# Casting the first 256 weight rows of the first feed-forward product last, behind ACT's seventh copy of the embedding projection

## The chip, the cores and the metric

The kernel runs on one core of a Trainium2 chip. A core has a matrix engine (TensorE, in the profile PE, with its weight loads as PEld), a vector engine (VectorE, DVE), an activation engine (ScalarE, ACT), a general engine (GpSimd, POOL) and an engine that here only issues transfers (SyncE, SP); all run their own instruction streams in order and wait for one another by semaphores. Transfers from memory (HBM) are issued by SP, ACT or POOL. The metric is the device time of one execution in microseconds (us), lower is better.

## The reference

One layer of a hybrid attention and recurrent block over 512 tokens of 1024 channels. What concerns us is its second half:

```python
h = layer_norm(DEEPNORM_ALPHA * h + merged @ w_out[l], ln1_g[l], ln1_b[l])
ff = jnp.square(jax.nn.relu(h @ w_ff1[l])) @ w_ff2[l]      # 1024 -> 4096 -> 1024
r = DEEPNORM_ALPHA * h + ff
r = r + jax.nn.sigmoid(r @ w_ple_gate[l]) * (p[l] @ w_ple_proj[l])
h = layer_norm(r, ln2_g[l], ln2_b[l])
```

The product `p[l] @ w_ple_proj[l]` (256 to 1024 channels, the embedding's projection) needs nothing of the layer's other results.

## The kernel before

Products in float32 are made of three matmuls in a reduced float32 format. An operand is split into a high part (a cast, on ACT) and a low part (operand minus high part, mostly on DVE); the product is high x high, high x low and low x high. The stationary operand of a matmul is loaded by a weight load (PEld) ahead of it.

The stretch around the change goes from the output projection (`po`) to the first feed-forward product. PE works, in this order, on the last block of the output projection, eight blocks of the embedding's projection (`ple_projection`, tile `ppw`, six matmuls each, two halves of columns times four blocks of tokens), mixed with transposes of the normed rows `r` (`hps`, by `h_factors`), and then the first product of the first feed-forward matrix. Each `ppw` block is copied by ACT (`pws`) and stored to a buffer in memory by SP (`pwd`). The eight blocks use a ring of three accumulator banks, but for the seventh, which has a bank of its own (`aux`).

`h_factors` makes the activations' factors out of the transposes: copies `hb` and `a22`, high parts `hc0H` to `hc6H` on ACT, low parts `hc0L` to `hc6L` and some sums on DVE. It is called for blocks 0 to 2 of tokens before the stretch, and for two halves of it (block 1 and block 3) inside it.

The first feed-forward product uses Strassen-like sums: columns of `w_ff1` go in four groups of 1024, and in each group seven products P1 to P7 take the place of eight. In the first group PE's order is P1, P2, P3, P5, P7, P6, P4. `w1_factor(t, n)` makes the factors of product n of group t: a weight tile `w1q` has 512 rows as four pieces of 128 partitions (k = 0 to 3) by 512 columns; for each pair of pieces ACT casts 1024 columns to the high part `w1h`, DVE subtracts to the low part `w1l`, and where a later product needs a sum of two weight quarters, POOL issues a transfer that adds the other quarter onto the pair in place (`W1_ADD`). P1 and P5 read the same tile: P5 reads it after P1's adds, P6 after P5's. P3 and P7 share a tile in the same way. The high and low parts have two buffers each, so a product's factors can be written when PE is through with the product two before.

The order of instructions on an engine is that of the program, but for operations that are put behind a named one (`tc.issue_after`); `queued` puts each operation of ACT and DVE in the feed-forward stage behind the last one that `queued` issued on the engine. In the kernel before, P1's factors are made when the fourth `pws` copy has been issued (`stored[0]`), in one piece:

```python
with tc.issue_after(normed[0].ins), tc.issue_after(stored[0].ins):
    w1 = w1_factor(0, P1)
```

`ff1` makes the matmuls of a product: for each of four blocks of 128 columns the 4 pieces k in order with the high weights, against the high and the low activations, and after all those the low weights.

Of the kernel before, what the change touches and what calls it, by code (L numbers as in the profile page):

```python
# [53 lines left out]
def f(ap):  # L54
    return ap.bitcast(F32)
# [3 lines left out]
def block_kernel(ctx: ExitStack, tc: tile.TileContext, t, out):  # L59
    nc = tc.nc  # L60
    te, ve, se, ge, sy = nc.tensor, nc.vector, nc.scalar, nc.gpsimd, nc.sync
# [8 lines left out]
    def open_pool(name, side=None, space=None, reuse="tile"):  # L70
        kw = {}
        if side:
            kw["side"] = side
        if space:
            kw["space"] = space
        cm = tc.tile_pool(name=name, bufs=1, reuse_waits=reuse, **kw)
        p = cm.__enter__()
        return p, (lambda: cm.__exit__(None, None, None))
# [26 lines left out]
    def gtile(name, dtype=F32R, n=None):  # L105

        if n is None:
            n = len(gplaces) % 4
            gplaces.append(n)
        return gpool.tile([P, 4, S], dtype, tag=f"g{n}", bufs=1, name=name)  # L110
# [249 lines left out]
    for i in range(1, NT):  # L360
        n = (i + 1) * P
# [136 lines left out]
    todo = list(dense)  # L498
# [286 lines left out]
    def half_product(ps, sh, sl, ws):  # L785

        for k, (wh, wl) in enumerate(ws):
            mm = mm3(ps, sh(k), sl(k), wh, wl, k == 0, k == len(ws) - 1)
        return mm

    def blocks(ws):
        return [(wh[:, k, :], wl[:, k, :]) for wh, wl in ws for k in range(2)]
# [49 lines left out]
    def queued(engine, op, *args, **kw):  # L842

        if engine in order_of:
            with tc.issue_after(order_of[engine].ins):
                order_of[engine] = getattr(engine, op)(*args, **kw)  # L846
        else:
            order_of[engine] = getattr(engine, op)(*args, **kw)

    order_of = {}  # L850
# [29 lines left out]
    P1, P2, P3, P4, P5, P6, P7 = range(7)  # L880
# [4 lines left out]
    def w1_rows(t, w):  # L885
        c = groups[t] * 1024 + w[1] * 512
        return w_ff1[w[0] * 512:(w[0] + 1) * 512, c:c + 512].rearrange("(k p) c -> p k c", p=P)

    def w1_load(t, w, issue=None):
# [14 lines left out]
        else:  # L904
            loads.append(sy.dma_start(tl, w1_rows(t, w)))

    W1_OF = {P1: B11, P2: B21, P3: B22, P5: B11, P7: B22, P6: B11, P4: B21}

    W1_ADD = {P1: B12, P5: B22, P3: B12}

    def w1_factor(t, n):

        tl = w1q[t, W1_OF[n]]
        hi, lo = (pools[1].tile([P, 4, 512], F32R, tag="w1" + x, bufs=2, name="w1" + x) for x in "hl")
        for k in (slice(0, 2), slice(2, 4)):
            queued(se, "copy", hi[:, k], tl[:, k])
            queued(ve, "tensor_sub", lo[:, k], tl[:, k], f(hi[:, k]))
            if n in W1_ADD:
                ge.dma_start(out=tl[:, k], in_=w1_rows(t, W1_ADD[n])[:, k], accum_op=OP.add)  # L919
        if n == P6:  # L920
            for k in (slice(0, 2), slice(2, 4)):
                queued(ve, "tensor_add", w1q[t, B21][:, k], w1q[t, B21][:, k], tl[:, k])
        return hi, lo
# [9 lines left out]
    pwss, projected, stored = [], [], []  # L933

    def ple_projection(i, hh):

        ps = (aux if (hh, i) == (1, 2) else acc)("ppw")
        tok = slice(i * P, (i + 1) * P)
        projected[:] = [half_product(ps, lambda k: pTH[:, k, tok], lambda k: pTL[:, k, tok], blocks(wp[hh:hh + 1]))]
        if i == 0:  # L940
            pwss.append(gtile("pws", F32))
        pws = pwss[hh][:, i]
        stored[:] = [se.copy(pws, ps)]
        sy.dma_start(pwd[:, i, hh * 512:(hh + 1) * 512], pws)

    todo = [(i, hh) for hh in range(2) for i in range(NT)]
# [3 lines left out]
    with tc.issue_after(normed[0].ins), tc.issue_after(stored[0].ins):  # L950
        w1 = w1_factor(0, P1)
# [4 lines left out]
    with tc.issue_after(projected[0].ins):  # L956
        h_factors(NT - 1)
    with tc.issue_after(turned[0].ins):
        for _ in range(2):
            ple_projection(*todo.pop(0))  # L960
    close_ln()
    close_hb()
    pools[0], close_fb = open_pool("fb", side="right")
# [93 lines left out]
    def rows_of(g, w):  # L1057
        return ff2_rows[w[0], g, :, :, w[1] * 512:(w[1] + 1) * 512]
# [14 lines left out]
    def add(g, tl, w):  # L1073
        return ge.dma_start(out=tl, in_=rows_of(g, w), accum_op=OP.add)  # L1074
# [18 lines left out]
    for k, (t_, n) in enumerate(seq):  # L1093
# [7 lines left out]
        if k + 1 < len(seq):  # L1101
            nxt = w1_factor(*seq[k + 1])
# [31 lines left out]
    late, close_late = open_pool("late", side="left")  # L1134
# [298 lines left out]
```

## Time and profile before

| what | value |
|---|---|
| time, median of 3 runs (lowest to highest) | 769.85 us (769.58 to 770.32) |
| the profiled execution's own time | 769.99 us |
| its span, first to last instruction | 768.3 us |
| PE busy | 757.8 us, 99% of the span |
| DVE, ACT, POOL busy | 596.7, 418.4, 268.1 us |
| mean granted clock of PE | 0.996 of full |

The span is what the trace covers; 1.7 us of the execution's own time lie outside it. All times of events are microseconds from the span's start. A busy share is an average over stages, so it is read by stage below. Matmuls overlap: one of 512 columns is shown 0.39 us long, but the next starts 0.23 us behind it.

### The profile page before, as it was taken

The page shows a single profiled execution, that of the slowest core. Times are in us where ns is not written, and L with a number is a line of the kernel's source. Part 1 is how long each engine was busy: PE and PEld are TensorE (multiplying, and loading weights), DVE is VectorE, ACT ScalarE, POOL GpSimd, SP SyncE. Part 2 cuts the span into 40 slices and gives each one's busy share as a digit, 9 for nine tenths or more (in the row PEclk, how much of TensorE's full clock was granted, in tenths as well). Part 3 has the DMA queues.
Part 4 walks back from the last instruction along what each step waited for, and adds up shares of the span by engine and source line. Part 5 has one row for each costly group of instructions (what it writes and reads, how often), then busy time and mean ns, then how long its engine had stood idle before and what let it go on. Part 6 is the DMA issues. An engine that isn't in the chain of part 4 may idle for free.

```text
span 768.3 us, 11493 instructions
## 1 busy us (share of the span) xinstructions
PE 757.8 (99%) x4332; PEld 663.2 (86%) x4332; DVE 596.7 (78%) x979; ACT 418.4 (54%) x637; POOL 268.1 (35%) x332
## 2 busy tenths in 40 slices
PE   8999999999999999999999999999999999999995
PEld 8788888889988888878889999999988888888885
DVE  7949999965557987585896767576888988998558
ACT  5546466697756633532366556656565465555210
POOL 6654554444255437470232121212010101126341
PEclk9999999999999999999999999999999999999998
DMA  8443233222223112372089996937497799895202
GB/s 283 127 131 83 56 82 83 83 69 68 71 67 92 62 44 81 91 289 101 1 243 200 335 249 191 238 84 129 112 223 192 144 402 305 140 184 186 93 27 110
DMA packets 77544, 110.43 MB, mean 144 GB/s; under 512 B 3248, under 2 KB 38576, under 8 KB 76208
## 3 DMA queue, kind: packets, MB, share of 16 engines
q1 hardware_dynamic: 58992, 72.76, 28.9%
q0 software_dynamic: 13920, 27.27, 20.6%
q10 hardware_dynamic: 4576, 9.67, 3.6%
q8 instruction: 34, 0.56, 0.3%
q14 instruction: 22, 0.18, 0.1%
HBM read 101.29 MB, written 8.39 MB: 143 GB/s over the span
## 4 chain that ended last, share of the span: by engine, by line
PE 94%; DVE 3%; issue 1%; POOL 1%; DMA 1%; DVEq 0%; ACT 0%; POOLq 0%
PE pf L993 21%; PE pf L1224 20%; PE pg L152 5%; PE pg L154 5%; PE pg L153 5%; PE pu L154 2%; PE pu L152 2%; PE pu L153 2%; PE po L152 2%; PE po L154 2%; PE po L153 2%; PE ptp L480 1%; PE kv L285 1%; PE mv L154 1%; PE mv L153 1%
## 5 line engine op out<-in xcount | busy, mean ns | idle before, releaser
L846 DVE TENSOR_TENSOR w1l<-w1q,w1h 128x1024 fp32r<-128x1024 f32 x55 | 65.0, 1222 | 34.8 <-ACT w1h L846 34.4
L846 DVE TENSOR_TENSOR wl<-b,wh 128x2048 fp32r<-128x2048 f32 x28 | 64.8, 2313 | 10.4 <-ACT wh L846 10.4
L846 ACT CAST w1h<-w1q 128x1024 fp32r<-128x1024 f32 x55 | 55.3, 1048 | 23.6 <-PE pf L993 20.6
L919 POOL DMA_DIRECT2D w1q<-in_w_ff x24 | 29.2, 1254 | 111.7 <-DVE w1l L846 108.4
L145 POOL TENSOR_TENSOR wgl<-wgr,wgh 128x256 fp32r<-128x256 f32 x64 | 49.9, 813 | 47.5 <-ACT wgh L142 47.5
L1074 POOL DMA_DIRECT2D b<-in_w_ff x14 | 17.9, 1279 | 133.3 <-DVE wl L846 125.6
L1224 PE MATMUL pf<-wh,ah 128*128 128x512 f32 x216 | 58.1, 391 | 0.0
L1224 PE MATMUL pf<-wh,al 128*128 128x512 f32 x216 | 57.8, 389 | 0.0
L846 ACT CAST wh<-b 128x2048 fp32r<-128x2048 f32 x28 | 53.5, 1909 | 3.2 <-DMA b<-in_w_ff 3.2
L1224 PE MATMUL pf<-wl,ah 128*128 128x512 f32 x216 | 53.5, 390 | 0.0
L154 PE MATMUL pg<-xH,wgl 128*128 128x512 f32 x128 | 50.6, 395 | 0.0
L152 PE MATMUL pg<-xH,wgh 128*128 128x512 f32 x128 | 50.4, 394 | 0.0
L153 PE MATMUL pg<-xL,wgh 128*128 128x512 f32 x128 | 50.3, 393 | 0.0
L1224 PEld LDWEIGHTS pf<-wh,al 128*128 128x128 f32 x216 | 40.6, 188 | 8.5
L1224 PEld LDWEIGHTS pf<-wh,ah 128*128 128x128 f32 x216 | 40.3, 188 | 8.7 <-ACT wh L846 0.4
L1224 PEld LDWEIGHTS pf<-wl,ah 128*128 128x128 f32 x216 | 40.5, 188 | 8.4
L145 POOL TENSOR_TENSOR wul<-wur,wuh 128x128 fp32r<-128x128 f32 x64 | 36.6, 605 | 19.0 <-ACT wuh L142 19.0
L846 DVE TENSOR_TENSOR c<-c,pf 128x512 f32<-128x512 f32 x48 | 30.5, 683 | 10.2 <-ACT c L846 10.2
L846 ACT ACTIVATE c<-c 128x1024 f32<-128x1024 f32 x12 | 12.7, 1061 | 31.3 <-DVE c L846 31.3
L767 POOL TENSOR_TENSOR lag<-lag,mhalf 128x1 f32<-128x1 f32 x8 | 7.5, 941 | 61.1 <-DVE lag L766 61.1
L153 PEld LDWEIGHTS pg<-xL,wgh 128*128 128x128 f32 x128 | 24.1, 188 | 4.6
L152 PEld LDWEIGHTS pg<-xH,wgh 128*128 128x128 f32 x128 | 24.1, 188 | 4.5
(396 smaller groups left out, 2297.1 us busy)
## 6 DMA issues: line engine op xcount, KB each, us to landing
b<-in_w_ff POOLq DMA_DIRECT2D x14, 1024.0 KB, 9.1
w1q<-in_w_ff POOLq DMA_DIRECT2D x24, 512.0 KB, 7.6
w1q<-in_w_ff SPq DMA_DIRECT2D x9, 1024.0 KB, 7.6
wgr<-in_w_in SPq DMA_DIRECT2D x16, 512.0 KB, 3.8
b<-in_w_ff SPq DMA_DIRECT2D x8, 1024.0 KB, 7.0
wor<-in_w_out SPq DMA_DIRECT2D x8, 512.0 KB, 7.3
b<-in_w_ff ACTq DMA_DIRECT2D x4, 1024.0 KB, 8.8
wpgr<-in_w_ple_gate SPq DMA_DIRECT2D x8, 512.0 KB, 9.1
```

Source lines behind the costliest of these rows:

```text
L145: (lo_eng or ge).tensor_sub(lo[:, k:k + n], raw[:, k:k + n], f(hi[:, k:k + n]))
L152: te.matmul(ps, sh, mh, start=first, stop=False, **kw)
L153: te.matmul(ps, sh, ml, start=False, stop=False, **kw)
L154: return te.matmul(ps, sl, mh, start=False, stop=last, **kw)
L285: te.matmul(b1[i][:, :208], (xH, xL, xH)[kind][:, k, i * P:(i + 1) * P], (wh, wh, wl)[kind], start=k == 0 and kind == 0, stop=k == KD - 1 ...
L480: te.transpose(ps[:, slot * P:(slot + 1) * P], prs[slot // 2][:, slot % 2, j * P:(j + 1) * P], ident)
L767: ge.tensor_tensor(out=ag[:, 3:4], in0=ag[:, 2:3], in1=mhalf[:, 0:1], op=OP.pow))
L846: order_of[engine] = getattr(engine, op)(*args, **kw)
L919: ge.dma_start(out=tl[:, k], in_=w1_rows(t, W1_ADD[n])[:, k], accum_op=OP.add)
L993: mm = te.matmul(ps, w[:, k, b * P:(b + 1) * P], a[:, k], start=fresh, stop=w is lo and k == 3, skip_group_check=True)
L1074: return ge.dma_start(out=tl, in_=rows_of(g, w), accum_op=OP.add)
L1224: mm = te.matmul(banks[n, s], (al if kind == 1 else ah)[:, q, tok], (wl if kind == 2 else wh)[:, q], start=fresh and kind == 0 and q == 0, ...
```

## The change

The casts, subtractions and adding transfers of P1 of the first group are split. The second pair of pieces (rows 256 to 511) is handled where P1's factors were made before. The first pair (rows 0 to 255) is handled in `finish`, which is called between the seventh and the eighth block of the embedding's projection and puts its cast behind ACT's copy of the seventh block. All later casts of the stage, P2's first, are queued behind that cast. The instructions are the same in number and shape.

```diff
+    late = []
...
-        for k in (slice(0, 2), slice(2, 4)):
+        def part(k):
             queued(se, "copy", hi[:, k], tl[:, k])
             queued(ve, "tensor_sub", lo[:, k], tl[:, k], f(hi[:, k]))
+
+        def add(k):
             if n in W1_ADD:
                 ge.dma_start(out=tl[:, k], in_=w1_rows(t, W1_ADD[n])[:, k], accum_op=OP.add)
+
+        if t == 0 and n == P1:
+
+            part(slice(2, 4))
+            add(slice(2, 4))
+
+            def finish(wait):
+                with tc.issue_after(wait.ins):
+                    order_of[se] = se.copy(hi[:, 0:2], tl[:, 0:2])
+                queued(ve, "tensor_sub", lo[:, 0:2], tl[:, 0:2], f(hi[:, 0:2]))
+                add(slice(0, 2))
+
+            late.append(finish)
+        else:
+            for k in (slice(0, 2), slice(2, 4)):
+                part(k)
+                add(k)
...
     with tc.issue_after(turned[0].ins):
-        for _ in range(2):
-            ple_projection(*todo.pop(0))
+        ple_projection(*todo.pop(0))
+        late.pop()(stored[0])
+        ple_projection(*todo.pop(0))
```

On ACT, from the first cast of P1 on, the rows of before are these (`w1h_4380` is P1's high part, `w1h_4476` P2's, `w1h_4530` P3's):

```order
L848 CAST w1h_4380<-w1q_4280 128x1024 [waits DMAHW2_49,Activation_49]
L846 CAST w1h_4380<-w1q_4280 128x1024
L846 CAST w1h_4476<-w1q_4312 128x1024 [waits DMAHW3_49,Activation_49]
L846 CAST w1h_4476<-w1q_4312 128x1024
L810 COPY hb1_3977<-hps1_4326 128x4x128 [waits PE_49]
L114 CAST hc1H_3949<-hps1_4326 128x4x128
L943 COPY pws_4397<-ppw_4390 128x512 [waits PE_49]
L943 COPY pws_4397<-ppw_4400 128x512 [waits PE_49]
L814 COPY a22_4419<-hps1_4410 128x512 [waits PE_49,Activation_49]
L114 CAST hc2H_3958<-hps1_4410 128x4x128
L943 COPY pws_4397<-ppw_4437 128x512 [waits PE_49]
L943 COPY pws_4397<-ppw_4446 128x512 [waits PE_49]
```

and of the change, up to the same last copy:

```order
L848 CAST w1h_4380<-w1q_4280 128x1024 [waits DMAHW2_49,Activation_49]
L810 COPY hb1_3977<-hps1_4326 128x4x128 [waits PE_49]
L114 CAST hc1H_3949<-hps1_4326 128x4x128
L964 COPY pws_4394<-ppw_4387 128x512 [waits PE_49]
L964 COPY pws_4394<-ppw_4397 128x512 [waits PE_49]
L814 COPY a22_4416<-hps1_4407 128x512 [waits PE_49,Activation_49]
L114 CAST hc2H_3958<-hps1_4407 128x4x128
L964 COPY pws_4394<-ppw_4434 128x512 [waits PE_49]
L932 CAST w1h_4380<-w1q_4280 128x1024
L846 CAST w1h_4476<-w1q_4312 128x1024 [waits DMAHW3_49,Activation_49]
L846 CAST w1h_4476<-w1q_4312 128x1024
L964 COPY pws_4394<-ppw_4446 128x512 [waits PE_49]
```

Three casts moved behind six copies and casts of the factors and the projection; the eighth copy now stands behind them.

On DVE the low parts of P1 and P2 (`w1l_4381`, `w1l_4477`) stood ahead of the factors of the last block of tokens:

```order
L848 TENSOR_TENSOR w1l_4381<-w1q_4280,w1h_4380 128x1024 [waits DMAHW2_49,Activation_49]
L846 TENSOR_TENSOR w1l_4381<-w1q_4280,w1h_4380 128x1024 [waits Activation_49]
L846 TENSOR_TENSOR w1l_4477<-w1q_4312,w1h_4476 128x1024 [waits DMAHW3_49,Activation_49]
L846 TENSOR_TENSOR w1l_4477<-w1q_4312,w1h_4476 128x1024 [waits Activation_49]
L120 TENSOR_TENSOR hc1L_3950<-hps1_4326,hc1H_3949 128x4x128 [waits PE_49,Activation_49]
L120 TENSOR_TENSOR hc2L_3959<-hps1_4410,hc2H_3958 128x4x128 [waits PE_49,Activation_49]
L817 TENSOR_TENSOR hps1_4410<-hps0_4409,a22_4419 128x512 [waits DVE_49]
L820 TENSOR_TENSOR hps2_4424<-hps1_4410,hb0_3976 128x512 [waits DVE_49]
L824 TENSOR_TENSOR hps0_4409<-hb0_3976,hps0_4409 128x512
L821 TENSOR_TENSOR hps3_4425<-hps2_4424,hb1_3977 128x512 [waits DVE_49]
```

and with the change:

```order
L848 TENSOR_TENSOR w1l_4381<-w1q_4280,w1h_4380 128x1024 [waits DMAHW2_49,Activation_49]
L120 TENSOR_TENSOR hc1L_3950<-hps1_4326,hc1H_3949 128x4x128 [waits PE_49,Activation_49]
L120 TENSOR_TENSOR hc2L_3959<-hps1_4407,hc2H_3958 128x4x128 [waits PE_49,Activation_49]
L817 TENSOR_TENSOR hps1_4407<-hps0_4406,a22_4416 128x512 [waits DVE_49]
L820 TENSOR_TENSOR hps2_4421<-hps1_4407,hb0_3976 128x512 [waits DVE_49]
L824 TENSOR_TENSOR hps0_4406<-hb0_3976,hps0_4406 128x512
L846 TENSOR_TENSOR w1l_4381<-w1q_4280,w1h_4380 128x1024 [waits Activation_49]
L821 TENSOR_TENSOR hps3_4422<-hps2_4421,hb1_3977 128x512 [waits DVE_49]
L846 TENSOR_TENSOR w1l_4477<-w1q_4312,w1h_4476 128x1024 [waits DMAHW3_49,Activation_49]
L846 TENSOR_TENSOR w1l_4477<-w1q_4312,w1h_4476 128x1024 [waits Activation_49]
```

P1's second subtraction and P2's two stand behind the factors' sums; POOL's transfer into rows 0 to 255 waits for the former.

On PE the order is the same; these are the rows of the change where P1 starts, the last of the eighth projection block ahead of it:

```order
L154 MATMUL ppw_4446<-wp_4277,pT_4264 128x512
L1015 MATMUL pf_4466<-hc0H_3947,w1h_4380 128x256 [waits Activation_49]
L1015 MATMUL pf_4466<-hc0H_3947,w1h_4380 128x256 x3
L1015 MATMUL pf_4466<-hc0L_3948,w1h_4380 128x256 x4
L1015 MATMUL pf_4466<-hc0H_3947,w1h_4380 128x256 x4
L1015 MATMUL pf_4466<-hc0L_3948,w1h_4380 128x256 x4
```

The first matmul of P1 (line 993 before, 1015 now) waits for ACT, now for the late cast.

## Rows read from the trace of the kernel before

**Rows 1.** The page: busy time, share of the span and instructions of each engine; and the engines' shares of the chain of work that ended last.

```profile
PE 757.8 (99%) x4332; PEld 663.2 (86%) x4332; DVE 596.7 (78%) x979; ACT 418.4 (54%) x637; POOL 268.1 (35%) x332
...
PE 94%; DVE 3%; issue 1%; POOL 1%; DMA 1%; DVEq 0%; ACT 0%; POOLq 0%
```

**Rows 2.** The chain that ended last in order of time, merged: start, length, engine, tile, line and count.

```profile
401.42 152.64 PE pf L993 x1296
```

**Rows 3.** The waits of weight loads from 401 us to the end, all of them: who waited for whom, us in total, times, longest.

```profile
PEld pf L1224 <- ACT wh L846: 0.4, 1, 0.4
```

**Rows 4.** Windows: stretch, its length, busy time and instructions of each engine in it, granted clock of PE, share of the DMA engines, GB/s; an early stretch and the two around the product's start.

```profile
4.00:8.00 4.00, 3.42 (x25) 3.24 (x25) 2.90 (x5) 2.41 (x5) 2.82 (x5) 1.00 0.94 337
...
390.00:400.00 10.00, 10.00 (x53) 8.32 (x53) 9.57 (x15) 8.13 (x13) 3.05 (x3) 1.00 0.66 217
400.00:410.00 10.00, 10.00 (x82) 9.76 (x81) 8.24 (x11) 7.88 (x14) 1.57 (x3) 1.00 0.97 223
```

**Rows 5.** PE's instructions in order of time: start, length, line, operation, output and inputs, count.

```profile
394.18 0.39 PE L154 MATMUL ppw<-wp,pT 128*128 128x512 f32 x1
394.41 0.60 PE L158 MATMUL hps<-ident,r 128*128 128x128 f32 x4
...
397.61 1.03 PE L158 MATMUL hps<-ident,r 128*128 128x128 f32 x8
...
399.65 0.40 PE L154 MATMUL ppw<-wp,pT 128*128 128x512 f32 x1
...
401.25 0.64 PE L993 MATMUL pf<-hc0H,w1h 128*128 128x256 f32 x4
...
405.02 2.05 PE L993 MATMUL pf<-hc0H,w1l 128*128 128x256 f32 x16
406.91 0.63 PE L993 MATMUL pf<-hc1H,w1h 128*128 128x256 f32 x4
```

**Rows 6.** The weight loads in order of time, the first of P1.

```profile
401.03 0.65 PEld L993 LDWEIGHTS pf<-hc0H,w1h 128*128 128x128 f32 x4
```

**Rows 7.** ACT's instructions in order of time; in brackets the idle time before one and what ended it.

```profile
394.60 0.58 ACT L943 COPY pws<-ppw 128x512 f32<-128x512 f32 x1 [0.80 <-PE ppw L154]
395.09 1.05 ACT L848 CAST w1h<-w1q 128x1024 fp32r<-128x1024 f32 x1
396.04 2.94 ACT L846 CAST w1h<-w1q 128x1024 fp32r<-128x1024 f32 x3
...
399.83 1.09 ACT L943 COPY pws<-ppw 128x512 f32<-128x512 f32 x2
400.79 0.62 ACT L814 COPY a<-hps 128x512 f32<-128x512 f32 x1
401.26 0.64 ACT L114 CAST hc2H<-hps 128x512 fp32r<-128x512 f32 x1
401.74 1.13 ACT L943 COPY pws<-ppw 128x512 f32<-128x512 f32 x2
...
405.27 2.00 ACT L846 CAST w1h<-w1q 128x1024 fp32r<-128x1024 f32 x2 [0.56 <-PE pf L993]
...
410.88 2.00 ACT L846 CAST w1h<-w1q 128x1024 fp32r<-128x1024 f32 x2 [1.18 <-PE pf L993]
...
426.04 1.05 ACT L846 CAST w1h<-w1q 128x1024 fp32r<-128x1024 f32 x1 [0.43 <-DMA w1q<-in_w_ff]
```

**Rows 8.** DVE's instructions in order of time.

```profile
396.31 1.22 DVE L848 TENSOR_TENSOR w1l<-w1q,w1h 128x1024 fp32r<-128x1024 f32 x1
...
401.93 0.69 DVE L120 TENSOR_TENSOR hc2L<-hps,hc2H 128x512 fp32r<-128x512 f32 x1 [0.40 <-ACT hc2H L114]
...
404.00 0.69 DVE L824 TENSOR_TENSOR hps<-hb,hps 128x512 f32<-128x512 f32 x1
...
407.17 2.36 DVE L846 TENSOR_TENSOR w1l<-w1q,w1h 128x1024 fp32r<-128x1024 f32 x2 [1.29 <-ACT w1h L846]
```

**Rows 9.** PE and its weight loads in order of time, at a wait for POOL early in the kernel.

```profile
29.68 0.39 PE L152 MATMUL iq<-iqwh,xH 128*128 128x512 f32 x1
...
30.14 0.19 PEld L153 LDWEIGHTS iq<-iqwl,xH 128*128 128x128 f32 x1 [0.49 <-POOL iqwl L145]
...
30.48 0.39 PE L154 MATMUL iq<-iqwh,xL 128*128 128x512 f32 x1
```

**Rows 10.** SP's transfers in order of time: the last five stores of the projection, and the load behind them.

```profile
395.21 8.85 SPq L944 DMA_DIRECT2D pwd<-pws  x5
421.92 0.38 SPq L903 DMA_DIRECT2D w1q<-in_w_ff  x1
```

**Rows 11.** POOL's adding transfers in order of time, those of P1 and of P3 (time to issue, not to land).

```profile
397.87 2.64 POOL L919 DMA_DIRECT2D w1q<-in_w_ff  x2 [3.06 <-DVE w1l L848]
408.93 2.40 POOL L919 DMA_DIRECT2D w1q<-in_w_ff  x2 [8.43 <-DVE w1l L846]
```

**Rows 12.** All adding transfers of POOL from 380 to 440 us (ns to issue, first and last start) and their time from issue to landing.

```profile
L919 POOL DMA_DIRECT2D w1q<-in_w_ff x8: 1176/1246/1531, 397.9 to 438.2; - x8
...
DMA to landing us min/median/max: 6.3/8.0/10.5
```

**Rows 13.** The time from issue to landing of P1's pair alone (issued at 397.87 and 399.0).

```profile
DMA to landing us min/median/max: 6.7/8.0/9.3
```

**Rows 14.** The same for P5's pair (issued at 414.4 and 415.5), whose second half P6's second cast waits for.

```profile
DMA to landing us min/median/max: 7.7/9.1/10.5
```

## The prediction

> **What bounds the kernel now.** I began with the page's busy times and the chain that ended last: PE is busy 757.8 us of the 768.3 us span and makes up 94% of the chain [rows 1]. What moves the end is therefore what makes PE wait. The chain in order of time then says where PE waits around the change: from 401.42 us on one unbroken piece of 152.64 us is PE in line 993, the first feed-forward product, and the list of weight-load waits after 401 us has one entry in all, 0.4 us in a later stage [rows 2, 3]. The windows show PE busy 10.00 of 10 us on both sides of the product's start, at a granted clock of 1.00 [rows 4]. So the stretch that the change edits has no idle time of PE to give back; ACT, by contrast, is busy about 8 of 10 us there.
>
> **Where everything stands.** On PE the eighth projection block gives way to P1, the first of seven products of the first group, at 401.25; its low part starts at 405.02, and P2 starts at 406.91, so one product takes 406.91 - 401.25 = 5.66 us [rows 5]. The first weight load of P1 starts at 401.03, behind the last weight load of the projection, with no wait shown [rows 6]. It reads rows 0 to 255 of P1's high weights (k = 0 first). Before, these were cast at 395.09 and were ready at 396.14, 4.9 us early [rows 7].
>
> **The change on ACT, step by step.** Nothing is removed or added; one cast of 1024 columns (1.05 us long, the next row starts 0.95 us behind it), its subtraction on DVE and its accumulating transfer on POOL move later, and P2's two casts go with them, since they are queued behind it. At 395.09 the other half of P1 is cast; at 396.04 ACT is free, and now takes the copy of the transposes made at 394.41 (these are done). From here on copies and casts of 512 columns follow one another at 0.48 us (399.83, then two, then 400.79; 401.26 is 0.47 on): hb at 396.04, hc1H at 396.52, the fifth copy at 397.00. The sixth copy waits for its product: the product's last matmul starts one spacing of 0.23 us ahead of the transposes at 397.61, so at 397.38, and a copy starts 0.42 us behind such a start (394.18 to 394.60), so 397.80. The copy to a22 waits for the eight transposes, which end at 397.61 + 1.03 = 398.64: start 398.70; hc2H at 399.18. At 399.66 ACT is free, but the seventh product's last matmul starts at 399.65, so the seventh copy starts at 399.65 + 0.42 = 400.07 and the late cast 0.49 us behind it, at 400.56. It ends at 401.61 [rows 5, 7]. An earlier ACT would not help, since two of these starts are set by PE.
>
> **What that does to PE.** The first weight load of P1 has to wait for that end. What follows a release by ACT starts 0.03 us later (hc2H ends at 401.26 + 0.64, its subtraction starts at 401.93 [rows 7, 8]), so I put the load at 401.65, against 401.03 before: 0.62 us late. How much of this PE loses is seen at an earlier stall: a weight load came at 30.14 after 0.49 us of idle, and the next matmul but one started at 30.48, where the spacing of 0.23 us from 29.68 on would have had it at 30.14: 0.34 us lost for about 0.45 us of lateness [rows 9]. The load normally runs about 0.1 us ahead of need. So PE loses 0.62 - 0.1 = 0.5 us. The bounds: 0.4 us if ACT turns round 0.1 us faster, 0.7 us if nothing of the lateness is hidden. All 48 matmuls of P1 (32 with high weights, 16 with low) and the six products behind it queue behind this load. Later products are paced by PE itself, the last stage on DVE (the 3% of the chain) follows PE's results, so the 0.5 us goes through to the end; at most the one later wait of 0.4 us, behind a transfer, could swallow it [rows 3].
>
> **The other things that move, and what covers them.** The third and fourth casts (P2) run at 401.51 to 403.5; P2 starts at 406.91 + 0.5: 3.9 us of cover. The eighth copy goes from 402.2 to 403.5 and its store on SP with it; the next thing on SP is a load at 421.92, so nothing waits [rows 7, 10]. P2's banks, freed by that copy, are needed at 407.4. On DVE hc1L and hc2L come earlier, with hc2L at 399.82 in place of 401.93; the sums behind it keep their spacing (the third starts 404.00 - 401.93 = 2.07 us behind hc2L and is 0.69 us long) and come to 402.5, where the late subtraction stands. Its cast is done by then. It takes 1.2 us, to 403.7; P1's low part needs it at 405.02 + 0.5. P2's subtractions end at 406.5 (needed at 411.2); P3's casts wait, as before, for P1's buffer (405.27 + 0.5, and for four casts of the factors, so 405.9), its subtractions slip from 407.17 to 408.9 and end at 411.3, needed at 405.02 + 2 x 5.66 + 0.5 = 416.8 [rows 5, 7, 8]. POOL's two adds for P3 slip with them from 408.93 to about 410.6, the second to 411.8; even at 10.5 us they land by 422.3, and P7, whose casts read them, starts at 401.25 + 4 x 5.66 + 0.5 = 424.4 [rows 5, 11, 12]. Each is paid from cover, so at nothing; the thinnest of them is the late subtraction's 1.8 us, and P7's second cast has 1.3 us if the slowest transfer comes; without that cover each late us would cost one.
>
> **The transfer is the thin place.** POOL's accumulating transfer into rows 0 to 255 was issued at 397.87, 0.34 us behind its subtraction's end at 397.53. It now starts at 403.7 + 0.34 = 404.04. P5's first cast reads these rows; before it started at 410.88, when PE had given its buffer back, so now at 411.4 [rows 7, 11]. Such transfers took 6.3 to 10.5 us, the first pair 6.7 and 9.3 us [rows 12 to 14]. So it lands between 410.3 and 414.5: hidden by 1 us, or late for the cast by up to 3.1 us, and P5 itself wants that cast by 401.25 + 3 x 5.66 + 0.5 = 418.7. I take 6.7 us (410.7), as the stores and the load that shared the first pair's time are out by then: no delay. The Trainium skill has a rule for the same path: its page "DMA: Bandwidth & Descriptors", section "Anatomy of one DMA — SWDGE (gpsimd) path", fits 2.0 us plus bytes over 436e3, which for 512 KB is an estimate of 3.2 us. By it the landing would be 407.2 and no lateness possible; the trace does not agree, its shortest such transfer took 6.3 us, so the rows decide and leave a rival.
>
> **The sum.** 769.99 us (the profiled execution, 0.14 us above the median of 769.85) + 0.5 = 770.5; beside the median it is 770.35. I say 770.4 us, 0.07% above. This kernel's measurement cannot tell less than about 0.2% (1.5 us) from no change.
>
> **The rivals.** First, a late transfer makes it slower. If the add lands late, P5's cast and its subtraction (1.2 us) are late, then POOL's two adds for P5, the second of which took 10.5 us and landed just when P6's second cast wanted it (0.43 us of wait at 426.04 [rows 7, 14]). P6 starts at 401.25 + 5 x 5.66 = 429.55, with the 0.5 us at about 430.05, and its third weight load (the first that reads rows 256 and up, two spacings of 0.12 us on) wants a cast of 1.05 us before it: the transfer has to land by 429.2. Back from there: issued by 418.7, the first of the pair 1.2 us earlier, P5's first subtraction started by 416.0, its cast by 414.9. So from a landing at 414.9, 10.9 us after issue, each late us costs one. For 771.5 us (over 0.2%) it must land about 1.1 us later still, at 12 us; 772.4 us at 13 us. Against it: the longest of eight was 10.5 us.
>
> Second, nothing is lost: the weight load waits less than I reckon, or the later 0.4 us wait takes the loss up: 769.9 to 770.1 us. For it speaks that one wait [rows 3]; against it that PE's own product sets the cast's start.
>
> Third, the clock falls at the gap. The early window, where PE is busy 3.42 of 4 us, so idle 0.58 us, has a granted clock of 1.00 [rows 4]; so I give it little. If one whole product ran at 1.2 GHz in place of 2.4 GHz it would cost up to its 5.66 us again: up to 776 us. [...]
>
> Fourth, it gets faster by more than 0.2%. PE has 0.4 us of waits after 401 us [rows 3], so even if the earlier factors removed all of it, 769.5 us would be the best; I have no mechanism for more.
>
> **How the numbers follow.** A loss of 0.4 to 0.7 us with all else hidden: 0.74. Nothing lost: 0.12. The late transfer beyond its cover: 0.09, of which 0.06 are over 771.4. The lower clock: 0.02. Faster for a reason I don't see: 0.03. So slower by over 0.2% has 0.08, faster 0.03, within 0.2% 0.89. The range takes in the bounds of the loss about both baselines, the case of nothing lost and the start of the late transfer: 769.7 to 771.3.
>
> **What would show it.** In the changed profile: ACT's late cast at about 400.6, directly behind the seventh copy; a wait of PE's weight load in line 1015 for ACT's cast of about 0.6 us, and the first P1 matmul at about 401.75; P2 5.66 us behind P1, no further wait in the seven products; the moved add issued at about 404 and P5's first cast at 411.4 behind PE, not behind a DMA. I am wrong if P1 starts at 401.25 as before, if P5, P7 or P6 show a wait of PE, or if the granted clock is under 1.00 in 400 to 410.

## The result, and the profile after

| | before | after |
|---|---|---|
| time, median of 20 runs each (lowest to highest) | 769.91 us (769.31 to 770.56) | 764.49 us (764.07 to 770.12) |
| ratio after to before | | 0.9941 (0.9931 to 0.9951) |

The change is 5.4 us faster, where I had said 770.4 us and no change that can be measured. The times of the changed kernel fall into two groups with nothing between: 17 runs at 764.07 to 764.98 us, and three at 770.09, 770.10 and 770.12. The profiled execution of the change is one of the three (770.09 us, span 768.4), so its trace shows the kernel as I had predicted it, and not where the 5.4 us come from. For the other group I ran the same kernel again (first experiment); its profile belongs to the faster group and is read here beside the first. Two executions beside the experiments, one of the kernel before (1539.66 us) and the fifth of the wait alone (1707.6 us), took twice the time of all others or more and are left out of every figure.

The page of the change, answering to [rows 1]: busy time of each engine, and the shares of the chain.

```profile
PE 758.0 (99%) x4332; PEld 663.2 (86%) x4332; DVE 596.0 (78%) x979; ACT 419.2 (55%) x637; POOL 270.2 (35%) x332
...
PE 94%; DVE 3%; POOL 1%; issue 1%; DMA 1%; ACT 0%; DVEq 0%; SPq 0%; POOLq 0%
```

Nothing stands out against before. The change in the slower group, in order of time: PE at the start of the first feed-forward product and at P2 [rows 5].

```profile
400.79 0.39 PE L154 MATMUL ppw<-wp,pT 128*128 128x512 f32 x1
401.43 0.74 PE L1015 MATMUL pf<-hc0H,w1h 128*128 128x256 f32 x4 [0.25 <-ACT w1h L932]
...
405.30 2.05 PE L1015 MATMUL pf<-hc0H,w1l 128*128 128x256 f32 x16
407.19 0.64 PE L1015 MATMUL pf<-hc1H,w1h 128*128 128x256 f32 x4
```

The same rows of the same kernel in the faster group:

```profile
400.43 0.39 PE L154 MATMUL ppw<-wp,pT 128*128 128x512 f32 x1
401.07 0.72 PE L1015 MATMUL pf<-hc0H,w1h 128*128 128x256 f32 x4 [0.25 <-ACT w1h L932]
...
404.80 1.98 PE L1015 MATMUL pf<-hc0H,w1l 128*128 128x256 f32 x16
406.62 0.62 PE L1015 MATMUL pf<-hc1H,w1h 128*128 128x256 f32 x4
```

Both wait alike for the late cast: P1's first matmul starts 0.64 us behind the projection's last one in both, where 0.23 us is the usual step. Then they part. The first four matmuls are shown 0.74 us long in the one and 0.72 in the other, sixteen 2.05 and 1.98; P2 comes 5.76 us behind P1 in the one and 5.55 in the other. The chain in order of time shows what this adds up to: start, length, tile, line and count, of the change in the slower group,

```profile
401.43 152.91 PE pf L1015 x1296
...
558.08 5.45 PE pf L1015 x48
```

and in the faster one, to be read against 152.64 us in [rows 2]:

```profile
401.07 147.15 PE pf L1015 x1296
...
551.95 5.45 PE pf L1015 x48
```

Before, the last 48 took longer:

```profile
557.78 5.66 PE pf L993 x48
```

In the faster group the same 1296 matmuls take 5.8 us less than in the slower one. Against before it is 5.7 us: the chain's piece of before begins 0.17 us behind its first matmul (401.42 against 401.25 in [rows 5]), so counted as in the other two it is 152.81 us. The 48 more behind a short other piece (their place in the last product) take 5.45 us in place of 5.66, in the slower group too. Together that is the whole gain. Nothing was waiting there: the windows of the two groups show PE busy 10.00 of 10 us at a granted clock of 1.00, as before [rows 4]. The slower group, then the faster (columns as in rows 4):

```profile
402.00:412.00 10.00, 10.00 (x87) 10.00 (x86) 9.02 (x11) 6.92 (x12) 2.78 (x3) 1.00 0.73 151
```

```profile
402.00:412.00 10.00, 10.00 (x91) 10.00 (x90) 8.66 (x11) 6.82 (x11) 3.15 (x3) 1.00 0.75 147
```

A PE that is busy all the time did 87 matmuls in 10 us in the one and 91 in the other. Where the difference is seen for one matmul is the line's groups by shape (count, shortest/median/longest in ns, first and last start). Before:

```profile
L993 PE MATMUL pf<-hc0L,w1h x64: 281/281/281, 401.7 to 523.6; 128*128 128x256 f32 x64
L993 PEld LDWEIGHTS pf<-hc0L,w1h x64: 187/188/192, 401.6 to 523.5; 128*128 128x128 f32 x64
```

and the change in the faster group:

```profile
L1015 PE MATMUL pf<-hc0L,w1h x64: 276/276/276, 401.6 to 518.9; 128*128 128x256 f32 x64
L1015 PEld LDWEIGHTS pf<-hc0L,w1h x64: 187/188/188, 401.5 to 518.8; 128*128 128x128 f32 x64
```

Every one of these 64 matmuls is shown 281 ns long before and 276 in the faster group. The starts say the same. These are the steps from one matmul's start to the next in ns, taken from the start times in the traces, from the projection's last one on (the first step is the one into P1):

```
before                  225  119 117 118 117 119
change, slower group    640  221 118 117 119
change, faster group    639  221 114 113 113
```

So the stage has **two paces**: 117.8 ns from matmul to matmul (401.25 to 553.78 us for 1295 steps), and 113.4 ns (401.07 to 547.94). The difference of 4.4 ns times the stage's 1344 matmuls is 5.9 us; less the 0.5 us that the wait costs, it is the 5.4 us measured.

The Trainium skill, page "TensorE: Matmul & The Clock Gate", section "Back-to-back issue gap", has columns over 2.4 GHz plus some 2.5 ns, which for 256 columns is an estimate of 109.2 ns, for matmuls by themselves; with a weight load for each, it says, both set the spacing. The rows show 113.4 and 117.8, so what is left above the page's figure is 4.2 or 8.6 ns.

### The profile page after: what moved, and what is told of

Same layout as the page of the kernel before. It is cut to its first block, busy times and chain, and to the rows that moved or that the text cites. A ratio compares the mean times of both kernels' runs of the same rounds, so it can differ in the third digit from the quotient of the medians.

```text
span 768.4 us, 11493 instructions
## 1 busy us (share of the span) xinstructions
PE 758.0 (99%) x4332; PEld 663.2 (86%) x4332; DVE 596.0 (78%) x979; ACT 419.2 (55%) x637; POOL 270.2 (35%) x332
## 4 chain that ended last, share of the span: by engine, by line
PE 94%; DVE 3%; POOL 1%; issue 1%; DMA 1%; ACT 0%; DVEq 0%; SPq 0%; POOLq 0%
PE pf L1015 21%; PE pf L1246 20%; PE pg L152 5%; PE pg L154 5%; PE pg L153 5%; PE pu L154 2%; PE pu L152 2%; PE po L154 2%; PE pu L153 2%; PE po L152 2%; PE po L153 2%; PE kv L285 1%; PE ptp L480 1%; POOL iqwl L145 1%; PE mv L154 1%; PE aq L153 1%
```

## The experiments

**The theories.** A, the pace: PE runs this stage at one of two paces, which one is settled when PE starts on it, and a wait of PE there, whatever causes it, mostly gives the quick one. B, the work: the order in which the factors are made, or the place of casts, subtractions and adding transfers, lets the products run more quickly. C, the clock: the pause changes what clock is granted. C needs no run: the granted clock is 1.00 in windows of both paces above. Nor does the pace follow the load on the transfers, as two stretches of the stage show (columns as in rows 4; first before, then the change in the faster group):

```profile
412.00:450.00 38.00, 38.00 (x325) 38.00 (x324) 24.94 (x28) 22.32 (x26) 7.22 (x6) 1.00 1.03 265
500.00:547.00 47.00, 47.00 (x401) 47.00 (x401) 32.83 (x36) 31.02 (x36) 7.23 (x6) 1.00 0.52 98
```

```profile
412.00:450.00 38.00, 38.00 (x337) 38.00 (x337) 26.28 (x29) 24.29 (x29) 7.69 (x7) 1.00 1.07 273
500.00:547.00 47.00, 47.00 (x417) 47.00 (x416) 36.76 (x38) 31.29 (x36) 7.33 (x7) 1.00 0.50 98
```

The share of the DMA engines halves from the first stretch to the second, and the steps stay: 117 to 119 ns in both before, 113 or 114 in both in the faster group. In the runs below, the pace of a profiled execution is read from its trace; that of the others is told from their times.

**The change again.** The kernel of the change, unchanged.

> The changed kernel as it is, to see the trace of a quick execution: 17 of its 20 runs took 764.1 to 765.0 us, three took 770.1, and the one that was profiled took 770.1. Theory A (pace): the matmuls of 256 columns of the first feed-forward product have two paces, 118 and 113 ns from start to start; which one holds is settled where PE starts the product, and it stays while PE runs unbroken. In a 764 us execution the piece from 401 us on is then paced at 113 to 114 ns and ends 1296 x 4.4 ns = 5.7 us earlier, with the same wait of 0.7 us for the late cast ahead of it. Theory B (place): the moved casts, subtraction and transfer free a shared port or the DMA engines; then the pace is 118 ns wherever nothing else runs, and gaps or long matmuls elsewhere are what is gone. Theory C (clock): the granted clock differs, visible as under 1.00 in slow executions.

764.39 us (763.94 to 764.99, five runs), ratio 0.9935 (0.9921 to 0.9948). The result repeats, and its profile, shown above, gave the two paces.

**The wait alone.** The kernel before, with one added copy of 64 columns of P1's first weights onto themselves, behind the seventh copy; nothing is moved.

```diff
-        for _ in range(2):
-            ple_projection(*todo.pop(0))
+        ple_projection(*todo.pop(0))
+        with tc.issue_after(stored[0].ins):
+            se.copy(w1[0][:, 0, 0:64], f(w1[0][:, 0, 0:64]))
+        ple_projection(*todo.pop(0))
```

> The kernel before with its casts, subtractions and transfers where they were; only 64 columns of P1's first high weights are rewritten in place (same values) by ACT behind the seventh projection copy, so that PE has to wait at the product's start: ACT reaches that at about 402.2 us and ends it at 402.4, so PE's first weight load comes 1.3 to 1.4 us late. Theory A: the wait alone gives the quick pace in most executions: 769.9 + 1.2 - 5.7 = 765.4 us. Theory B: 769.9 + 1.2 = 771.1 us, at 118 ns.

764.65 to 765.70 us in four of five runs (the fifth is the one of 1707.6 us), ratio 0.9945 (0.9932 to 0.9959). Its waits behind 401 us (who for whom; us, times, longest), and the chain:

```profile
PEld pf L995 <- ACT w1h L961: 1.6, 1, 1.6
PE pf L995 <- ACT w1h L961: 1.2, 1, 1.2
```

```profile
401.84 147.16 PE pf L995 x1296
```

This PE waits 1.2 us where before it waited for nothing, and the kernel is over 4 us faster. B has nothing to stand on here, since the factors are made in the old order.

**The move without the wait.** The change, with the late cast one copy earlier.

```diff
+    late.pop()(stored[0])
     with tc.issue_after(projected[0].ins):
         h_factors(NT - 1)
     with tc.issue_after(turned[0].ins):
-        ple_projection(*todo.pop(0))
-        late.pop()(stored[0])
-        ple_projection(*todo.pop(0))
+        for _ in range(2):
+            ple_projection(*todo.pop(0))
```

> The change with the late part behind the sixth projection copy in place of the seventh: cast, subtraction and transfer still move (the cast to about 398.3 us, the transfer to about 400), but the cast ends by 399.4, ahead of PE's need at 401, so PE does not wait. Theory A: no wait, pace 118 ns as before, 769.9 us. Theory B: about 764 us without any wait of PE.

769.9 us (769.39 to 770.57, 11 runs), ratio 1.0005 (0.9996 to 1.0013). ACT's late cast, and the chain:

```profile
398.10 1.05 ACT L932 CAST w1h<-w1q 128x1024 fp32r<-128x1024 f32 x1
```

```profile
401.23 152.64 PE pf L1015 x1296
```

The cast is over 2 us before PE wants it, PE doesn't wait, and the pace is that of before to the hundredth, with the moved work still moved.

**A longer wait.** The change, with the late cast behind both last blocks of the projection.

```diff
-        ple_projection(*todo.pop(0))
+        for _ in range(2):
+            ple_projection(*todo.pop(0))
         late.pop()(stored[0])
-        ple_projection(*todo.pop(0))
```

> The change with the late part behind the eighth copy: the cast ends at about 402.75 us, so PE's wait grows by 1.3 us over the change's. Theory A: quick pace, 764.4 + 1.3 = 765.7 us, unless the pace depends on how long the wait is, then 771.1 us or a mix. Theory B: 765.7 us as well, or less.

765.75 us (765.32 to 766.51, five runs), ratio 0.9952 (0.9939 to 0.9964). Waits, then the chain:

```profile
PEld pf L1015 <- ACT w1h L932: 2.0, 1, 2.0
PE pf L1015 <- ACT w1h L932: 1.6, 1, 1.6
```

```profile
403.12 147.17 PE pf L1015 x1296
```

The wait grew by 1.3 us of PE against the change, the kernel by 1.4 us (765.75 - 764.39), and the pace stayed the quick one. So the wait is a price, and what it buys doesn't grow with it.

**A smaller wait.** The change, with only piece k = 0 (512 columns) cast late; k = 1 goes with the early ones. (Later expectations call this run e7.)

```diff
         if t == 0 and n == P1:
+            part(slice(1, 2))
             part(slice(2, 4))
...
-                    order_of[se] = se.copy(hi[:, 0:2], tl[:, 0:2])
-                queued(ve, "tensor_sub", lo[:, 0:2], tl[:, 0:2], f(hi[:, 0:2]))
+                    order_of[se] = se.copy(hi[:, 0:1], tl[:, 0:1])
+                queued(ve, "tensor_sub", lo[:, 0:1], tl[:, 0:1], f(hi[:, 0:1]))
```

> The change with half as much cast late: of rows 0 to 255 only 0 to 127 (512 columns, 0.6 us in place of 1.05) wait for the seventh copy, rows 128 to 255 are cast early. The late cast then ends at about 400.95 us, 0.45 us sooner, and PE's first weight load is only 0.15 to 0.2 us late, PE hardly idle. If so short a wait is enough for the quick pace: 764.0 to 764.2 us; if not, 769.9 us or a mix of both.

763.68 us (763.37 to 763.89, four runs), ratio 0.9918 (0.9905 to 0.9931). The one wait there, and the chain:

```profile
PEld pf L1016 <- ACT w1h L933: 0.2, 1, 0.2
```

```profile
401.36 146.97 PE pf L1016 x1296
```

The weight load waits 0.2 us and PE loses about 0.1 us (a step of 207 ns in place of 113), yet the pace is the quick one. That is 6 us under the kernel before; by less than 1 us it is also under the change, which is too little for these runs to tell. The same kernel once more:

> The kernel of e7 once more, for its time and for how often it runs at 113.4 ns: its four runs took 763.4 to 763.9 us, but the change itself had three slow draws in twenty. If the short wait settles the quick pace each time: 763.7 us in all; if it is drawn as with the longer waits: about one run in six at 769.5 us.

764.04 us (763.78 to 764.10, five runs), ratio 0.9924 (0.991 to 0.9937). In both sets together all nine were quick.

**No wait at all, by size.** As in the smaller wait, but only 128 of the columns of k = 0 are cast late and the other 384 early.

```diff
+            queued(se, "copy", hi[:, 0, 128:512], tl[:, 0, 128:512])
...
-                    order_of[se] = se.copy(hi[:, 0:1], tl[:, 0:1])
+                    order_of[se] = se.copy(hi[:, 0, 0:128], tl[:, 0, 0:128])
```

> As e7, but only 128 columns of P1's first weights (one column block of rows 0 to 127) are cast behind the seventh copy, the other 384 early. All casts, subtractions and transfers stand where they stand in e7; the late cast takes some 0.3 us and ends at about 400.8 us, ahead of the need at 401.0, so PE's weight load does not wait. If the wait settles the pace: 118 ns, 769.8 us. If e7's gain comes of the order of casts: 763.7 us.

769.77 us (769.49 to 769.98, 11 runs), ratio 0.9997 (0.9988 to 1.0006). ACT's last short cast, and the chain:

```profile
400.69 0.30 ACT L934 CAST w1h<-w1q 128x128 fp32r<-128x128 f32 x1
```

```profile
401.55 152.64 PE pf L1017 x1296
```

The cast still stands behind the seventh copy, but it ends at 400.99, in time; with the wait the gain is gone. What decides is not the place in the order but whether PE has to wait.

**A different instruction in place of the wait.** The kernel before, with one short matmul of 64 columns ahead of P1 whose result P1 overwrites.

```diff
+        if (t, n) == (0, P1):
+            mms.append(te.matmul(w1_banks(t, n)[0][:, 0:64], ah[:, 0, 0:P], ah[:, 0, 0:64], start=True, stop=True,
+                                 skip_group_check=True))
```

> The kernel before with one more matmul of 64 columns on PE ahead of the first product, into the bank that the product then overwrites; its operands are long ready, so PE does not wait. If the quick pace needs a wait of PE: 118 ns, 770.0 us. If any irregular step in PE's order is enough: 113.4 ns, 764.1 us.

769.6 us (769.4 to 770.26, 11 runs), ratio 0.9997 (0.9989 to 1.0006); the chain:

```profile
401.11 152.72 PE pf L996 x1296
...
557.57 5.45 PE pf L996 x48
```

This odd step in an unbroken stream doesn't do what a wait does: the 1296 keep the slow pace. It isn't without effect, since the last 48 take 5.45 us where the kernel before takes 5.66. No other odd step was tried.

**A wait midway.** The kernel before, with two copies of 64 columns onto themselves, put on ACT so that P1 of the third group finds its first weights late (the first copy holds the second back until PE has read the product before). (The expectation of the run after it calls this run e5.)

```diff
+        if (t_, n) == (2, P1):
+            queued(se, "copy", prev[1][:, 3, 448:512], f(prev[1][:, 3, 448:512]))
+            queued(se, "copy", w1[0][:, 0, 0:64], f(w1[0][:, 0, 0:64]))
...
-        w1 = nxt
+        prev, w1 = w1, nxt
```

> The kernel before, untouched at the stage's start; ahead of the first product of the third group (at about 480 us) ACT rewrites 64 columns of the last product's low weights in place, which it can do only when PE is through with them, and then 64 columns of the next product's first high weights, so that PE waits some 0.6 us there. Theory A (pace settled by a wait): 118 ns up to 480 us, 113.4 ns behind it: 672 matmuls x 4.4 ns = 3.0 us less, 769.9 + 0.5 - 3.0 = 767.4 us. If only the stage's start matters: 770.4 us.

Six runs: 770.43, 767.25, 767.51, 767.6, 767.86, 768.08 us, ratio 0.997 (0.9958 to 0.9982). Five are some 2 us faster than before, which is 672 matmuls (half the stage) times 4.4 ns = 3.0 us, less a wait of the kind seen here. The profiled one is the other, 770.43 us. Its waits and its chain:

```profile
PEld pf L993 <- ACT w1h L846: 0.7, 1, 0.7
PE pf L993 <- ACT w1h L846: 0.5, 1, 0.5
```

```profile
401.06 76.54 PE pf L993 x650
...
480.72 73.76 PE pf L993 x624
```

624 matmuls in 73.76 us are 118 ns each: PE waited, and kept the slow pace. So a wait doesn't set the quick pace; it draws anew: the same wait leaves one pace in one execution and the other in the next. The two traces of the change say the same, since they part behind steps that agree to 1 ns (640 and 639, then 221 and 221).

**Both waits.** The change, with the midway wait as well. If a wait draws anew, this one should now and then throw a quick stage back.

> The change plus the wait midway of e5. If a wait brings the quick pace, or leaves it: 764.4 + 0.5 = 764.9 us with 113.4 ns on both sides, and executions that began at 118 ns are mended from 475 us on (then about 767.5 us). If a wait throws the pace anew: some at 118 ns behind 475 us, about 767.9 us.

Six runs: 768.28, 765.01, 765.58, 765.56, 765.43, 765.9 us, ratio 0.9948 (0.9937 to 0.9959). The profiled one is the first, 2.7 us above the others' median; waits and chain:

```profile
PEld pf L1015 <- ACT w1h L846: 0.9, 1, 0.9
PEld pf L1015 <- ACT w1h L932: 0.7, 1, 0.7
```

```profile
401.78 74.05 PE pf L1015 x651
...
478.95 73.76 PE pf L1015 x624
```

651 matmuls at 113.7 ns (with the wait's odd step), then a wait of 0.9 us of the weight load, and 624 at 118 ns. One kernel in one execution shows both paces, and the wait stands between them; the same wait can cost 2.7 us.

**What the runs settle.** Of the 33 experimental runs in which PE never waited in this stage (the move without the wait, the short matmul, the eighth), the 20 of the kernel before shown above and 47 more of it taken beside the experiments, none was quick: the lowest is 769.15 us. Of the runs with a wait at the start and none midway, 17 of 20, five of five, four of four, five of five and nine of nine were: 40 of 43. B is refuted in both directions, by the wait without the move and by the moves without the wait. A stands, with the correction that the wait draws, and the quick pace is only the likelier draw. What in the chip makes two paces, and what decides a draw, no run here shows.

## Why the prediction was wrong

**The step that failed** is the one sentence "Later products are paced by PE itself", taken with 5.66 us per product: I carried the spacing of before over as a constant of the shape. It is one of two values, and the change redraws it. With 5.45 us (48 times 113.4 ns) in its place, 28 products give 28 x 0.21 = 5.9 us, and the sum is 769.99 + 0.5 - 5.9 = 764.6, beside 764.49 measured. From the same step came the fourth rival's bound: "PE has 0.4 us of waits ... I have no mechanism for more". Idle time of PE bounds the gain only if busy PE can't be quicker, and [rows 4], 10.00 of 10 us, didn't say that. That rival, at 0.03, is what happened.

**The clock, third rival.** It could not have been this: the granted clock is 1.00 at both paces.

**What held.** In the profiled run of the change the projection's last matmul starts at 400.79; 0.23 us on, at 401.02, P1 would have started, against 401.25 in [rows 5], so this trace is 0.23 us early. ACT in it:

```profile
400.33 1.05 ACT L932 CAST w1h<-w1q 128x1024 fp32r<-128x1024 f32 x1
401.28 2.00 ACT L846 CAST w1h<-w1q 128x1024 fp32r<-128x1024 f32 x2
...
411.77 2.00 ACT L846 CAST w1h<-w1q 128x1024 fp32r<-128x1024 f32 x2 [2.97 <-DMA w1q<-in_w_ff]
...
426.33 1.05 ACT L846 CAST w1h<-w1q 128x1024 fp32r<-128x1024 f32 x1 [0.45 <-DMA w1q<-in_w_ff]
```

The late cast, which stands behind seven copies and casts and not six as said above the prediction, was forecast at 400.56; it is at 400.33, or 400.56 with the shift. The waits behind 401 us, all of weight loads and of PE:

```profile
PEld pf L1015 <- ACT w1h L932: 0.7, 1, 0.7
PEld pf L1246 <- ACT wh L846: 0.5, 1, 0.5
PE pf L1015 <- ACT w1h L932: 0.3, 1, 0.3
```

The weight load waits 0.7 us (0.62 forecast). PE's loss is read from the starts: 401.43 - 401.02 = 0.41 us, and the next step is 221 ns in place of 118, 0.10 more: 0.51 us, where I had 0.5. So the second rival, that nothing is lost, is out too. The later wait that could have swallowed the loss is 0.5 us, beside 0.4 before: it swallowed nothing.

**The moved work on DVE and POOL**, in the same trace:

```profile
402.27 1.22 DVE L846 TENSOR_TENSOR w1l<-w1q,w1h 128x1024 fp32r<-128x1024 f32 x1
```

```profile
403.80 1.21 POOL L923 DMA_DIRECT2D w1q<-in_w_ff  x1 [4.79 <-DVE w1l L846]
```

The late subtraction was put at 402.5 and the add at 404.04; with the shift both are there. The transfer was the thin place, and there my choice was off: P5's first cast starts at 411.77 (412.00 with the shift) behind the transfer, not at 411.4 behind PE. From the transfer's issue to the cast that waited for it passed 7.97 us, where I took 6.7 from bounds of 6.3 to 10.5. P5 doesn't notice, nor does P6, whose second cast waits 0.45 us as against 0.43 before: PE waits nowhere else in the stage. So the first rival was right in that the add lands late for the cast, and wrong in that it decides anything; the 10.9 us that it needed were not reached.

## What to carry to other kernels

A bound from idle time ("PE is 99% busy, so there is nothing to gain") holds only for the pace that the busy engine has; read the steps from start to start too, and compare them with those of the same shape elsewhere or in other runs. Where times of one kernel fall into two groups, one profile shows one group: look at which, before explaining with it. A long unbroken stage of equal matmuls may be worth a small wait at its head, tried and measured over enough runs, since here a weight load's wait of 0.2 us went with a gain of 6 us in nine of nine runs, and a wait midway once cost 2.7.

## What was not expected of the hardware

Equal matmuls of 256 columns, each with its weight load, at a granted clock of 1.00, keep in this stage one of two paces (117.8 or 113.4 ns) for 150 us on end, with no wait and no idle time of PE in either. The weight loads differ too, as the groups above hint (187/188/192 and 187/188/188): away from the waits a third of them is shown 192 ns long at the slow pace (397 of 1190 before), and none at the quick one. Without a wait the pace changes, in these traces, only at another shape, and there the traces show a regularity. Between the 1296 and the last 48 stand 16 matmuls of 512 columns, whose steps go by some 231 and 236 ns in turn. In all twelve traces the last 48 are slow where the last of these steps is 231, and quick where it is 235 or 236:

```
                        last three steps   the 48 behind    the 1296 ahead
before                  231 236 231        118 118 117      slow
move without the wait   231 235 231        119 117 118      slow
an eighth as late       231 236 231        118 117 118      slow
change, slower group    236 231 236        118 114 113      slow
short matmul            236 231 235        119 113 113      slow
change, faster group    236 231 236        118 114 113      quick
half as late            236 230 236        119 113 113      quick
```

(the other five, with waits of 1.2 and 1.6 us, the two with a wait midway and half as late once more, go as the last four). One reading of this is a phase of some 5 ns that a run of equal matmuls carries along and that a wait resets; no run sets such a phase, so it is not shown. The profiled run of the change had the slow pace for 1296 and the quick one for the last 48. What the phase is taken against, and why no run of the kernel before drew the quick one, stays open.
